# Recurrence weights split and rows squared during attention's first part, with five orders of loads, matmuls and tests changed

## The chip, the cores and the metric

The kernel runs on one core of a Trainium2 chip. The core has a matrix engine (TensorE, PE in the profile; PEld is its loading of weights), VectorE (DVE), ScalarE (ACT), GpSimd (POOL) and SyncE (SP), which here issues nearly all DMA transfers, from one queue in order. The metric is the device time of one execution in microseconds (us); lower is better.

## The reference

One decoder layer on 2048 tokens of 1024 features, in float32. The input is normalized and goes through one projection whose columns belong to three groups; their outputs are concatenated, projected, normalized and added to the input.

```python
hn = rms_norm(x, g_pre)
proj = hn @ w_in
rg_x, rg_g, da_q, da_k, da_v, da_g, xa_q, xa_g = jnp.split(proj, cuts, axis=-1)
xc = causal_depthwise_conv(rg_x, conv_w, conv_b)
y_rg = rg_lru(xc, w_rg_a, b_rg_a, w_rg_x, b_rg_x, lru_lambda) * jax.nn.silu(rg_g)
...
o = diff_attention(q, k, v, lam)
o = rms_norm(o, g_subln) * (1.0 - LAMBDA_INIT)
y_da = o.reshape(b_, s, DA_W) * jax.nn.silu(da_g)
oc = mem_cross_attention(xa_q.reshape(b_, s, XA_HEADS, XA_HEAD_DIM), km, vm)
y_xa = oc.reshape(b_, s, XA_W) * jax.nn.silu(xa_g)
y = jnp.concatenate([y_rg, y_da, y_xa], axis=-1) @ w_out
x = x + rms_norm(y, g_post)
```

`rg_lru` is a gated linear recurrence: two sigmoid gates from block-diagonal weights, then a scan along the tokens. `diff_attention` is causal, with 4 heads, two softmaxes per head of which one is subtracted with weight lambda. `mem_cross_attention` attends into 256 memory tokens.

## The kernel before

**Products in three parts.** A float32 operand is split into a high part in TensorE's rounded format and a low part, the rest. `split_weight` does this for weights: ScalarE copies the high part (L238), VectorE or GpSimd subtracts it (L239). `mm3` then runs three matmuls (high x high, low x high, high x low), each recorded by L198; transposes are L202.

**Projection.** The columns of `w_in` are grouped in 16 pairs of two 128-column blocks: eight of attention (qk, v, g), four of cross-attention (xa), four of the recurrence (rg). `project` runs twice: for chunks 0 and 1 of the 512-token chunks (the first half, pairs in their own order, so the rg pairs are pairs 12 to 15), then for chunks 2 and 3 (the second half, order `ORDER_B`, where rg pairs stand among the others). A pair is four blocks of 24 matmuls. In the first half each weight piece (four per pair) is loaded as `wraw`, split into `wp`, and stored to DRAM as `WD`; the second half loads `WD`. `w_conv` asks for pieces four or more ahead.

**Recurrence.** For each rg pair and chunk `ev_rg` evacuates the convolution's input (ScalarE, L592), convolves on VectorE (L597, L600), splits the result into `xchl` (VectorE L603, GpSimd L604), and makes the SiLU gate `rgg` (ScalarE, then VectorE L610). A little later `rg_gates` runs the gate matmuls `rgo`, their sigmoids on ScalarE, and the scan on VectorE (L637).

**Attention** is woven between the projection's matmuls by generators: `s_stream` makes scores and exponentials (`e`, in 12 buffers of the pool `pe`), weights and adds the two softmaxes (GpSimd L765, VectorE L766); `t_stream` transposes them (`pt`), splits them (ScalarE L806, VectorE L807) and multiplies by the values. `subln` normalizes each head with a matmul by ones. The order on PE is fixed by the program: a counter of recorded matmul time decides which generator goes next. The orders of the other engines and of the DMA queue come from a scheduler that follows dependences, buffers and priorities.

**Rows of x.** Chunk 0 is loaded and normalized first, and its transposes are woven with the first matmuls (`woven`). Rows of chunk 1 (`xrows`) and of the memory (`memx`) are loaded right behind it. Rows of chunks 2 and 3 are loaded at pair 13 (`next_x`), squared and summed on ScalarE (L283), and scaled on VectorE (L291).

**Output projection.** After the second half, `load_wout` splits the output weights in three groups (`woraw` to `wout` or `wo`); the token loop multiplies (`po`) in the order of groups 0, 2, 1.

Of the kernel before, what the change touches and what calls it, by code (L numbers as in the profile page):

```python
# [57 lines left out]
def hybrid_layer(  # L58
# [66 lines left out]
    ones_r = const.tile([128, 128], F32R, name="ones_r")  # L125
# [16 lines left out]
    def setup():  # L142
# [10 lines left out]
        nc.vector.tensor_scalar(ones_r, ident, 0.0, 1.0, op0=ALU.mult, op1=ALU.add)  # L153
# [164 lines left out]
    MEM0, WB0 = 8, 80  # L318
    wraw, wcv = {}, {}

    def w_load(*ids):
        for i in ids:
            if i < WB0:
                wraw[i] = praw.tile([128, 512], F32, tag="raw", name="wraw")
                nc.sync.dma_start(wraw[i], wsrc[i])

    def w_conv(*ids, eng=nc.gpsimd, pool=pw):
        for i in ids:
            if i < len(wsrc) and i not in wcv:
                w = wcv[i] = f4("wp", (128, 2, 2, 256), F32R, pool)  # L330
                if i >= WB0:

                    q = ORDER_B[(i - WB0) // 4]
# [5 lines left out]
                if not MEM0 <= i < MEM0 + 16:  # L339
                    q = i if i < MEM0 else i - 16  # L340
                    store(lambda w=w, q=q: nc.sync.dma_start(
                        WD[q // 4][q % 4], asf(w).rearrange("p a b c -> p (a b c)")), 4.0)
# [33 lines left out]
    for i in range(4):  # L376
        nc.sync.dma_start(xb[:, i].rearrange("p a b -> p (a b)"), x[CH + i * 128:CH + (i + 1) * 128, :])
    mrows = load_rows(mem, 2, "memx")
# [5 lines left out]
    def woven(c, rows):  # L384
# [6 lines left out]
        for kb in range(KB):  # L391
# [6 lines left out]
            if c == 0:  # L398
                if kb in (1, 2, 4, 6):
# [214 lines left out]
    def rg_gates(b, c, xc, xh, gs):  # L614
# [5 lines left out]
        ri = f4("ri", (128, 2, CH))  # L620
        for g in range(2):
            o = ps_s("rgo")
            mm3(o, state["rgh"][:, b, g, :], state["rgl"][:, b, g, :], xh[:, 0], xh[:, 1], True, True)
# [74 lines left out]
    def s_stream(jobs):  # L698

        q2s = {}  # L700

        def q2_load(i):
            if i < 2 * len(jobs) and i not in q2s:
                h, pr = jobs[i // 2]
                if has("qk", h, pr // 4):
                    q2s[i] = load_q2(h, 2 * pr + i % 2)
        due = now[0]
        for ij, (h, pr) in enumerate(jobs):
# [3 lines left out]
            while kready.get((h, pr // 4), 1e9) > now[0]:  # L712
# [119 lines left out]
    def subln(h, pr, A, B):  # L832
        c, j = divmod(pr, 2)
        s = ps_t("ss", (128, 256))
        mm(s, ones_r, B[:, 0, :], True, False)
        mm(s, ones_r, B[:, 1, :], False, True)
# [80 lines left out]
    xn = {}  # L917

    def next_x():
# [9 lines left out]
        for c in (2, 3):  # L929
            spawn(norm_steps(xn[c], SQ_GAP), 6.0 if c == 2 else 20.0)  # L930
# [8 lines left out]
    def start_b():  # L939
# [5 lines left out]
        (2, 0): start_attention,  # L945
        (13, 0): next_x,
# [12 lines left out]

    def load_wout(grp):  # L960
# [18 lines left out]
    project((2, 3), 80, ORDER_B, {(0, 0): start_b, (15, 2): last_pair})  # L979
# [118 lines left out]
```

## Time and profile before

| | |
|---|---|
| time, median of 3 runs (lowest to highest) | 1470.88 us (1470.23 to 1471.95) |
| the profiled execution's own time | 1467.53 us |
| its span, first to last instruction | 1465.7 us |
| TensorE matmuls busy | 1412.3 us, 96% |
| TensorE weight loads | 1199.2 us, 82% |
| VectorE, ScalarE, GpSimd busy | 61%, 53%, 33% |
| mean granted clock of TensorE | 0.994 |
| DMA | 234.37 MB, mean 160 GB/s |

Matmuls are pipelined and overlap the weight loads, so the two rows of TensorE don't add. A busy share is a mean over stages with different limits: what a stage is limited by is read from the waits in that stage. The granted clock is 1.00 at full speed (2.4 GHz) and 0.50 at the lower level (1.2 GHz).

### The profile page before, as it was taken

To read this page: it belongs to the slowest core of one execution; us is meant where nothing else is said; L and a number is where in the kernel's file an instruction comes from. 1 tells how busy PE (TensorE), PEld (TensorE's weight loads), DVE (VectorE), ACT (ScalarE), POOL (GpSimd) and SP (SyncE) were. 2 spreads that over 40 slices of the span, in tenths; PEclk is the share of its full clock that TensorE was granted. 3 is DMA by queue.
4 is the path that set the end of the run, shared out by engine and by line. 5 is a ranking of instruction groups with operands and counts; after the bars stand their busy time and mean duration, and the time that the engine had idled before them with its cause. 6 is when DMAs were issued, how large, how long until landed. Compare 5 with 4: busy or idle time off the path is not lost.

```text
span 1465.7 us, 21854 instructions
## 1 busy us (share of the span) xinstructions
PE 1412.3 (96%) x7568; PEld 1199.2 (82%) x7568; DVE 898.3 (61%) x1872; ACT 775.9 (53%) x1900; POOL 477.3 (33%) x568
## 2 busy tenths in 40 slices
PE   5999999999999899999999999999999999999997
PEld 3798889888887678888887898888877888888886
DVE  6531555676644876746547666757678777767222
ACT  6343544666547784745555545555566545554221
POOL 2031333344435632412213222212255333334221
PEclk9999999999999999999999999999999999999999
DMA  8689787745433348356324554232475334322231
GB/s 298 180 263 338 230 240 237 247 143 181 166 119 110 134 163 247 121 173 196 114 97 118 165 177 168 86 113 70 143 251 169 101 135 150 102 76 94 87 122 72
DMA packets 147870, 234.37 MB, mean 160 GB/s; under 512 B 12464, under 2 KB 82224, under 8 KB 147760
## 3 DMA queue, kind: packets, MB, share of 16 engines
q1 hardware_dynamic: 147616, 232.98, 48.8%
q8 instruction: 59, 0.97, 0.3%
q14 instruction: 51, 0.42, 0.1%
q10 hardware_dynamic: 144, 0.01, 0.0%
HBM read 142.76 MB, written 90.18 MB: 159 GB/s over the span
## 4 chain that ended last, share of the span: by engine, by line
PE 73%; DVE 9%; ACT 7%; DMA 4%; POOL 3%; issue 3%; SPq 1%; DVEq 0%; POOLq 0%; ACTq 0%
PE ip L198 36%; PE po L198 16%; PE s L198 7%; PE o L198 6%; PE pt L202 3%; PE xas L198 2%; DVE e L766 1%; DVE nm L740 1%; PE xao L198 1%; DMA q<-QD 1%; DVE xc L600 1%; PE rgo L198 1%; ACT e L742 1%; PE xat L202 1%; POOL e L765 1%
## 5 line engine op out<-in xcount | busy, mean ns | idle before, releaser
L198 PE MATMUL ip<-hnT,wp 128*128 128x512 f32 x2688 | 680.5, 397 | 6.9 <-DVE rgg L610 2.6
L198 PEld LDWEIGHTS ip<-hnT,wp 128*128 128x128 f32 x2688 | 496.0, 190 | 109.8 <-DVE hnT L307 4.5
L742 ACT ACTIVATE e<-s,nm 128x512 f32<-128x512 f32 (+3 forms) x320 | 200.1, 626 | 254.7 <-DVE nm L740 235.8
L740 DVE TENSOR_REDUCE nm<-s 128x1 f32<-128x512 f32 (+3 forms) x320 | 193.4, 605 | 37.4 <-PE s L198 33.1
L198 PE MATMUL po<-wout,yg 128*128 128x512 f32 x768 | 193.4, 393 | 5.0 <-POOL wout L239 2.4
L765 POOL TENSOR_SCALAR e<-e,f 128x512 f32<-128x512 f32 (+3 forms) x160 | 121.3, 773 | 235.5 <-DVE f L761 161.6
L198 PE MATMUL s<-kv,q 128*128 128x512 f32 (+3 forms) x640 | 182.9, 367 | 3.9 <-DMA q<-QD 2.4
L198 PEld LDWEIGHTS po<-wout,yg 128*128 128x128 f32 x768 | 141.1, 188 | 35.4 <-POOL wout L239 4.2
L766 DVE SCALAR_TENSOR_TENSOR e<-e,f 128x512 f32<-128x512 f32 (+3 forms) x160 | 138.0, 887 | 29.9 <-POOL e L765 29.7
L807 DVE TENSOR_TENSOR pthl<-pt,pthl 128x512 fp32r<-128x512 f32 (+1 forms) x144 | 94.5, 656 | 68.0 <-ACT pthl L806 67.5
L198 PE MATMUL o<-pthl,kv 128*128 128x256 f32 (+1 forms) x864 | 134.3, 290 | 1.0 <-DVE pthl L807 0.9
L198 PEld LDWEIGHTS s<-kv,q 128*128 128x128 f32 x640 | 114.5, 189 | 25.1 <-DMA q<-QD 3.0
L239 POOL TENSOR_TENSOR wp<-wraw,wp 128x512 fp32r<-128x512 f32 x67 | 91.1, 1368 | 127.1 <-ACT wp L238 110.8
L198 PEld LDWEIGHTS o<-pthl,kv 128*128 128x128 f32 x864 | 114.1, 189 | 4.5 <-DVE pthl L807 1.8
L806 ACT CAST pthl<-pt 128x512 fp32r<-128x512 f32 (+1 forms) x144 | 80.7, 561 | 55.2 <-PE pt L202 54.5
L239 POOL TENSOR_TENSOR yg<-yraw,yg 128x512 fp32r<-128x512 f32 x48 | 64.2, 1341 | 132.8 <-ACT yg L238 122.4
L198 PE MATMUL ip<-wp,hnT 128*128 128x256 f32 x768 | 99.7, 284 | 1.3 <-POOL wp L239 0.8
L198 PEld LDWEIGHTS ip<-wp,hnT 128*128 128x128 f32 x768 | 95.8, 191 | 3.0 <-POOL wp L239 1.0
L198 PE MATMUL po<-wo,yg 128*128 128x512 f32 x384 | 97.2, 392 | 0.0
L202 PE MATMUL pt<-ident,e 128*128 128x128 f32 x544 | 83.0, 272 | 3.3 <-DVE pthl L807 3.3
L198 PEld LDWEIGHTS po<-wo,yg 128*128 128x128 f32 x384 | 71.0, 188 | 14.3
L202 PEld LDWEIGHTS pt<-ident,e 128*128 128x128 f32 x544 | 66.9, 140 | 18.4 <-DVE pthl L807 3.8
(188 smaller groups left out, 1686.1 us busy)
## 6 DMA issues: line engine op xcount, KB each, us to landing
WD<-wp SPq DMA_DIRECT2D x64, 512.0 KB, 4.7
wp<-WD SPq DMA_DIRECT2D x64, 512.0 KB, 4.3
wraw<-in_w_in_dram SPq DMA_DIRECT2D x64, 256.0 KB, 3.4
q<-QD SPq DMA_DIRECT2D x128, 128.0 KB, 3.7
kv<-KD SPq DMA_DIRECT2D x24, 512.0 KB, 5.9
kv<-VD SPq DMA_DIRECT2D x24, 512.0 KB, 6.2
yraw<-YD SPq DMA_DIRECT2D x48, 256.0 KB, 2.7
QD<-qkhl SPq DMA_DIRECT2D x32, 256.0 KB, 3.5
```

What stands on the lines that cost most here:

```text
L198: nc.tensor.matmul(o, w, xx, start=start, stop=stop)
L202: nc.tensor.transpose(o, i, ident)
L239: eng.tensor_sub(lo, raw, asf(hi))
L600: nc.vector.scalar_tensor_tensor(xc[:, 0:CH], xr[:, k:k + CH], vec2[:, cw + k:cw + k + 1], xc[:, 0:CH], op0=ALU.mult, op1=ALU.add)
L740: nc.vector.tensor_reduce(out=nm[:, c, kc:kc + 1], in_=s[:, 0:w], op=ALU.max, axis=AX.X, negate=True)
L742: nc.scalar.activation(e[kc, c][:, 0:w], s[:, 0:w], AF.Exp, bias=nm[:, c, kc:kc + 1], accum_out=l[:, c, kc:kc + 1])
L765: nc.gpsimd.tensor_scalar(e2, e2, f[:, 1, kc:kc + 1], 1.0, op0=ALU.mult, op1=ALU.mult)
L766: nc.vector.scalar_tensor_tensor(e1, e1, f[:, 0, kc:kc + 1], e2, op0=ALU.mult, op1=ALU.add)
L806: nc.scalar.copy(hi[:, 0:n], t[:, 0:n])
L807: nc.vector.tensor_sub(lo[:, 0:n], t[:, 0:n], asf(hi[:, 0:n]))
```

## The change

1. **A new stage, `ahead`**, starts at pair 4 of the first half and takes three of the 12 `e` buffers until it ends. In each of 16 steps it loads one weight piece of the rg pairs and half a row block of chunks 2 and 3, splits the piece (ScalarE and GpSimd), stores both parts to `WD`, and squares and sums the row half on ScalarE. The rg pairs of the first half then load their pieces from `WD`. In `next_x` the rows of chunks 2 and 3, loaded again, are only scaled (`scale_rows`).
2. **The ones** of `subln` become one column, read 128 times.
3. **The start:** rows of chunk 1 are loaded during the fourth step of the first woven block, those of the memory behind that block.
4. **The gates' matmuls:** both gates' products with the high part run first, then both with the low part.
5. **Scores** of a job wait until 6.5 us of recorded time after its first query load.
6. **Output weights:** the four raw loads of group 2 are issued in the last quarter of the last pair, into free buffers.

```diff
-    ones_r = const.tile([128, 128], F32R, name="ones_r")
+    ones_r = const.tile([128, 1], F32R, name="ones_r")
...
-    MEM0, WB0 = 8, 80
+    MEM0, RG0, WB0 = 8, 64, 80
...
             if i < len(wsrc) and i not in wcv:
                 w = wcv[i] = f4("wp", (128, 2, 2, 256), F32R, pool)
-                if i >= WB0:
-
-                    q = ORDER_B[(i - WB0) // 4]
+                if i >= RG0:
+
+                    q = ORDER_B[(i - WB0) // 4] if i >= WB0 else (i - 16) // 4
                     nc.sync.dma_start(asf(w).rearrange("p a b c -> p (a b c)"), WD[q][i % 4])
                     continue
...
-    for i in range(4):
-        nc.sync.dma_start(xb[:, i].rearrange("p a b -> p (a b)"), x[CH + i * 128:CH + (i + 1) * 128, :])
-    mrows = load_rows(mem, 2, "memx")
+    mrows = []
...
             if c == 0:
+                if kb == 3:
+                    for i in range(4):
+                        t0 = CH + i * 128
+                        nc.sync.dma_start(xb[:, i].rearrange("p a b -> p (a b)"), x[t0:t0 + 128, :])
...
             w_conv(7, pool=p4)
+            mrows.extend(load_rows(mem, 2, "memx"))
...
+        os = [ps_s("rgo") for _ in range(2)]
         for g in range(2):
-            o = ps_s("rgo")
-            mm3(o, state["rgh"][:, b, g, :], state["rgl"][:, b, g, :], xh[:, 0], xh[:, 1], True, True)
+            mm(os[g], state["rgh"][:, b, g, :], xh[:, 0], True, False)
+            mm(os[g], state["rgl"][:, b, g, :], xh[:, 0], False, False)
+        for g in range(2):
+            o = os[g]
+            mm(o, state["rgh"][:, b, g, :], xh[:, 1], False, True)
...
                     q2s[i] = load_q2(h, 2 * pr + i % 2)
+                    landed[i] = now[0] + 6.5
...
-            while kready.get((h, pr // 4), 1e9) > now[0]:
+            while max(kready.get((h, pr // 4), 1e9), landed[2 * ij]) > now[0]:
...
-        mm(s, ones_r, B[:, 0, :], True, False)
-        mm(s, ones_r, B[:, 1, :], False, True)
+        ones = ones_r.to_broadcast([128, 128])
+        mm(s, ones, B[:, 0, :], True, False)
+        mm(s, ones, B[:, 1, :], False, True)
...
+    def ahead():
+
+
+        ssx = const.tile([128, 8, 2], F32, name="ssx")
+        while room["e"] < 3:
+            yield 0.4
+        room["e"] -= 3
+        for k in range(16):
+            raw = f2("wahead", (128, 512), F32R, pe)
+            nc.sync.dma_start(asf(raw), w_in[48 + k])
+            row = f2("xahead", (128, 512), pool=pe)
+            t0, j = 2 * CH + (k // 2) * 128, k % 2
+            nc.sync.dma_start(row, x[t0:t0 + 128, j * 512:j * 512 + 512])
+            yield 6.0
+            hi = f2("whi", (128, 512), F32R, pe)
+            nc.scalar.copy(hi, asf(raw))
+            nc.gpsimd.tensor_sub(raw, asf(raw), asf(hi))
+            yield 2.5
+            nc.scalar.activation(row, row, AF.Square, accum_out=ssx[:, k // 2, j:j + 1])
+            yield 1.0
+            for i, t in enumerate((hi, raw)):
+                nc.sync.dma_start(WD[12 + k // 4][k % 4][:, i * 512:i * 512 + 512], asf(t))
+            yield 3.5
+        room["e"] += 3
+        nc.gpsimd.tensor_add(rx, ssx[:, :, 0], ssx[:, :, 1])
+        rsqrt_mean(rx, rx, D)
+
+    def scale_rows(c):
+        for i, row in enumerate(xn[c]):
+            for p in row:
+                nc.vector.tensor_scalar_mul(p, p, rx[:, 4 * (c - 2) + i:4 * (c - 2) + i + 1])
+                yield SQ_GAP
...
-            spawn(norm_steps(xn[c], SQ_GAP), 6.0 if c == 2 else 20.0)
+            spawn(scale_rows(c), 6.0 if c == 2 else 20.0)
...
+        (4, 0): lambda: spawn(ahead()),
...
+    def last_raw():
+        for kb in range(4):
+            wo_load(2, kb)
+
+    project((2, 3), 80, ORDER_B, {(0, 0): start_b, (15, 2): last_pair, (15, 3): last_raw})
```

Three places show how the scheduler's lists move. The first is ScalarE in the rg pairs of the first half, about one chunk of one pair: `xr` is the convolution's input, `rgg` the SiLU gate, `rgo` and `ri` the two sigmoid gates, `junk` the squares, `wp` the weight splits. Before:

```order
L283 ACTIVATE junk,ss<-xrow 128x512 x2
L592 COPY xr<-ip 128x512
L238 CAST wp<-wraw 128x512
L283 ACTIVATE junk,ss<-xrow 128x512
L238 CAST wp<-wraw 128x512
L251 ACTIVATE rs<-rsv 128x4
L283 ACTIVATE junk,ss<-xrows 128x512
L252 ACTIVATE rs<-rs 128x4
L283 ACTIVATE junk,ss<-xrows 128x512
L260 ACTIVATE rgg<-ip 128x512
L283 ACTIVATE junk,ss<-xrows 128x512
L261 ACTIVATE rgg<-rgg 128x512
```

And in the changed kernel, from one pair's gates to the next:

```order
L637 ACTIVATE rga<-ri,nsp_249 128x512
L596 COPY xr<-ip 128x512
L638 ACTIVATE ri<-ri,nsp_250 128x512
L642 ACTIVATE ri<-ri,tinyb 128x512
L643 ACTIVATE ri<-ri 128x512
L260 ACTIVATE rgg<-ip 128x512
L261 ACTIVATE rgg<-rgg 128x512
L262 ACTIVATE rgg<-rgg 128x512
L260 ACTIVATE ri<-rgo,nbias 128x512 x2
L261 ACTIVATE ri<-ri 128x512 x2
L262 ACTIVATE ri<-ri 128x512 x2
```

The squares and the weight copies between the steps of the recurrence are gone; the gates' exponentials, logarithms and inverses follow each other in twos.

The second place is SP's DMA queue where attention begins, about 150 us into the span: `q` are query loads, `WD` weight stores, `GD` the store of an attention gate. Before:

```order
L341 DMA WD_180<-wp 128x1024
L325 DMA wraw<-in_w_in_dram 128x512
L692 DMA q_1711<-QD_98 128x2x128 x2
L341 DMA WD_181<-wp 128x1024
L325 DMA wraw<-in_w_in_dram 128x512
L506 DMA GD_151<-gs 128x512
L692 DMA q_1770<-QD_99 128x2x128 x2
```

And in the changed kernel:

```order
L328 DMA WD_180<-wp 128x1024
L325 DMA wraw<-in_w_in_dram 128x512
L939 DMA wahead<-in_w_in_dram 128x512
L942 DMA xahead<-in_x_dram 128x512
L328 DMA WD_181<-wp 128x1024
L700 DMA q_1721<-QD_98 128x2x128 x2
L510 DMA GD_151<-gs 128x512
L325 DMA wraw<-in_w_in_dram 128x512
L700 DMA q_1776<-QD_99 128x2x128 x2
```

The first two loads of the new stage and the second weight store now stand ahead of the first pair of query loads.

The third place is VectorE in the second half, about 766 to 777 us into the span: `xc` is the convolution, `e` the weighted sum of exponentials, `nm` the maxima of scores, `pthl` the split of transposed exponentials, `ri<-rga,carry,ri` the scan. Before:

```order
L766 SCALAR_TENSOR_TENSOR e<-e,f 128x512 x2
L740 TENSOR_REDUCE nm<-s 128x1
L766 SCALAR_TENSOR_TENSOR e<-e,f 128x512
L597 TENSOR_SCALAR xc<-xr,vec_243 128x512
L637 SCALAR_TENSOR_TENSOR ri<-rga,carry,ri 128x512
L740 TENSOR_REDUCE nm<-s 128x1
L600 SCALAR_TENSOR_TENSOR xc<-xr,vec_243,xc 128x512
L640 TENSOR_TENSOR ri<-ri,rgg 128x512
L600 SCALAR_TENSOR_TENSOR xc<-xr,vec_243,xc 128x512
L807 TENSOR_TENSOR pthl<-pt,pthl 128x512
```

And in the changed kernel:

```order
L601 TENSOR_SCALAR xc<-xr,vec_243 128x512
L775 SCALAR_TENSOR_TENSOR e<-e,f 128x512
L604 SCALAR_TENSOR_TENSOR xc<-xr,vec_243,xc 128x512
L749 TENSOR_REDUCE nm<-s 128x1
L604 SCALAR_TENSOR_TENSOR xc<-xr,vec_243,xc 128x512
L816 TENSOR_TENSOR pthl<-pt,pthl 128x512
L604 SCALAR_TENSOR_TENSOR xc<-xr,vec_243,xc 128x512
L749 TENSOR_REDUCE nm<-s 128x1
L607 CAST xchl<-xc 128x512
L775 SCALAR_TENSOR_TENSOR e<-e,f 128x512
L645 SCALAR_TENSOR_TENSOR ri<-rga,carry,ri 128x512
L816 TENSOR_TENSOR pthl<-pt,pthl 128x512
```

The convolution's first step moved ahead of a sum, and the scan moved from ahead of the first `pthl` to behind it.

## Rows read from the trace of the kernel before

**Rows 1.** Page, busy us (share of the span) and instructions of the engines

```profile
PE 1412.3 (96%) x7568; PEld 1199.2 (82%) x7568; DVE 898.3 (61%) x1872; ACT 775.9 (53%) x1900; POOL 477.3 (33%) x568
```

**Rows 2.** PE's waits by what ended them: us in total, times, longest

```profile
PE po L198 <- POOL wout L239: 2.4, 4, 0.7
PE po L198 <- ACT wout L238: 1.5, 1, 1.5
```

**Rows 3.** Timeline of PE: start, us, line, op, [idle before <-releaser]

```profile
480.67 0.73 PE L198 MATMUL rgo<-xchl,rgh 128*128 128x512 f32 x2 [1.40 <-POOL xchl L604]
487.45 8.45 PE L198 MATMUL ip<-hnT,wp 128*128 128x512 f32 x36 [1.25 <-DVE rgg L610]
511.16 0.73 PE L198 MATMUL rgo<-xchl,rgh 128*128 128x512 f32 x2 [1.16 <-POOL xchl L604]
```

**Rows 4.** Windows of 12 us: PE, PEld, DVE, ACT, POOL busy, clock, DMA, GB/s

```profile
478.00:490.00 12.00, 9.21 (x31) 6.49 (x30) 10.64 (x14) 11.44 (x26) 6.79 (x11) 0.86 0.55 188
773.00:785.00 12.00, 8.65 (x43) 6.91 (x42) 8.94 (x16) 8.22 (x19) 1.46 (x2) 0.86 0.39 122
```

**Rows 5.** Windows by stage, columns as in rows 4

```profile
150.00:455.00 305.00, 301.44 (x1665) 259.84 (x1665) 183.25 (x410) 170.75 (x431) 120.94 (x150) 1.00 0.60 193
455.00:515.00 60.00, 53.40 (x214) 41.30 (x213) 44.24 (x54) 45.39 (x100) 34.18 (x43) 0.95 0.37 126
515.00:1050.00 535.00, 527.34 (x2879) 450.65 (x2878) 349.40 (x690) 300.32 (x716) 139.16 (x185) 1.00 0.45 145
...
150.00:200.00 50.00, 50.00 (x241) 41.78 (x241) 28.51 (x63) 23.91 (x59) 17.39 (x20) 1.00 0.84 246
```

**Rows 6.** Groups by form, 455 to 515 us: xcount | busy us, mean ns

```profile
L600 DVE SCALAR_TENSOR_TENSOR xc<-xr,vec,xc 128x512 f32<-128x512 f32 x12 | 14.0, 1168 | 0.4
L239 POOL TENSOR_TENSOR wp<-wraw,wp 128x512 fp32r<-128x512 f32 x6 | 9.0, 1512 | 0.4 <-ACT wp L238 0.3
L283 ACT ACTIVATE junk<-xrow 128x512 f32<-128x512 f32 x8 | 5.0, 626 | 0.0
```

**Rows 7.** The same view, VectorE alone, 560 to 800 us

```profile
L600 DVE SCALAR_TENSOR_TENSOR xc<-xr,vec,xc 128x512 f32<-128x512 f32 x24 | 18.8, 784 | 0.4
```

**Rows 8.** Timeline of SP's queue and of PE, first query blocks

```profile
145.65 0.81 PE L198 MATMUL s<-kv,q 128*128 128x256 f32 x2 [2.38 <-DMA q<-QD]
...
152.42 0.94 SPq L692 DMA_DIRECT2D q<-QD  x2
...
160.48 0.62 PE L198 MATMUL s<-kv,q 128*128 128x512 f32 x2
```

**Rows 9.** Page, costliest groups: VectorE's weighted sum of exponentials

```profile
L766 DVE SCALAR_TENSOR_TENSOR e<-e,f 128x512 f32<-128x512 f32 (+3 forms) x160 | 138.0, 887 | 29.9 <-POOL e L765 29.7
```

**Rows 10.** Timeline of SP's queue and of ScalarE at the output projection

```profile
1083.92 10.68 SPq L969 DMA_DIRECT2D woraw<-in_w_out_dram  x5
...
1091.68 1.14 ACT L238 CAST wout<-woraw 128x512 fp32r<-128x512 f32 x2 [0.63 <-DMA woraw<-in_w_out_dram]
```

**Rows 11.** Timeline of GpSimd, VectorE and PE at 777 us

```profile
769.97 1.74 POOL L636 TENSOR_TENSOR ri<-ri 128x512 f32<-128x512 f32 x1
...
771.87 0.94 DVE L597 TENSOR_SCALAR xc<-xr,vec 128x512 f32<-128x512 f32 x1 [1.31 <-POOL xr L591]
776.43 0.68 DVE L807 TENSOR_TENSOR pthl<-pt,pthl 128x512 fp32r<-128x512 f32 x1
...
777.16 0.66 PE L202 MATMUL pt<-ident,e 128*128 128x128 f32 x4 [3.35 <-DVE pthl L807]
```

**Rows 12.** Timeline of VectorE and PE at the start

```profile
12.57 0.68 DVE L239 TENSOR_TENSOR wp<-wraw,wp 128x512 fp32r<-128x512 f32 x1
31.54 1.89 DVE L291 TENSOR_SCALAR memx<-memx,rs 128x512 f32<-128x512 f32 x2
...
34.15 1.19 PE L198 MATMUL ip<-hnT,wp 128*128 128x512 f32 x4 [1.38 <-DVE hnT L307]
```

**Rows 13.** Weight loads of the ones: duration ns min/median/max, first and last start

```profile
L198 PEld LDWEIGHTS ss<-sq,ones_r x64: 187/188/192, 172.1 to 1385.6; 128*128 128x128 f32 x64
```

More of the change, by code (lines that the diff above doesn't have):

```diff
@@ L152, in setup @@
         nc.vector.memset(tinyb, 1e-37)
-        nc.vector.tensor_scalar(ones_r, ident, 0.0, 1.0, op0=ALU.mult, op1=ALU.add)
+        nc.vector.tensor_scalar(ones_r, ident[:, 0:1], 0.0, 1.0, op0=ALU.mult, op1=ALU.add)
     def setup2():
@@ L322, in w_load, with w_store @@
         for i in ids:
-            if i < WB0:
+            if i < RG0:
                 wraw[i] = praw.tile([128, 512], F32, tag="raw", name="wraw")
                 nc.sync.dma_start(wraw[i], wsrc[i])
+    def w_store(w, q, delay):
+        store(lambda: nc.sync.dma_start(WD[q // 4][q % 4], asf(w).rearrange("p a b c -> p (a b c)")), delay)
     def w_conv(*ids, eng=nc.gpsimd, pool=pw):
@@ L339, in w_conv @@
                 if not MEM0 <= i < MEM0 + 16:
-                    q = i if i < MEM0 else i - 16
-                    store(lambda w=w, q=q: nc.sync.dma_start(
-                        WD[q // 4][q % 4], asf(w).rearrange("p a b c -> p (a b c)")), 4.0)
+                    w_store(w, i if i < MEM0 else i - 16, 4.0)
     def load_rows(src, n, name):
@@ L698, in s_stream @@
     def s_stream(jobs):
-        q2s = {}
+        q2s, landed = {}, {}
         def q2_load(i):
@@ L917, in hybrid_layer @@
     xn = {}
+    rx = const.tile([128, 8], F32, name="rx")
+    def ahead():
[27 more added lines that the diff above has]
+                yield SQ_GAP
     def next_x():
@@ L957, in y_granule, with wo_load @@
         return g
+    woraw = {}
+    def wo_load(grp, kb):
+        if (grp, kb) not in woraw:
+            raw = woraw[grp, kb] = f4("woraw", pool=pw if grp == 2 and kb == 3 else p4)
+            nc.sync.dma_start(raw, w_out[4 * grp + kb])
+        return woraw[grp, kb]
     def load_wout(grp):
@@ L967, in load_wout @@
         for kb in range(4):
-            raw = f4("woraw")
-            nc.sync.dma_start(raw, w_out[4 * grp + kb])
+            raw = wo_load(grp, kb)
             for j in range(2):
@@ L977, in last_pair @@
         load_wout(0)
-    project((2, 3), 80, ORDER_B, {(0, 0): start_b, (15, 2): last_pair})
+    def last_raw():
+        for kb in range(4):
+            wo_load(2, kb)
+    project((2, 3), 80, ORDER_B, {(0, 0): start_b, (15, 2): last_pair, (15, 3): last_raw})
     def y_ready(tt, grp):
```

## Prediction

> **What bounds the kernel now.** I read the busy times first: TensorE's matmuls stand at 1412.3 of 1465.7 us [rows 1], so some 53 us are idle. The change leaves the matmuls as they are, but for a few that change places, so it can only move waits. The table of PE's waits says which are large: 2.4 + 1.5 us, for instance, at the output projection's weights [rows 2]. The third reading was the timeline of PE through the last four pairs of the first half, the recurrence pairs: six waits of 0.5 to 1.4 us in 60 us, ended by VectorE or GpSimd, three of which stand in [rows 3]. There the clock matters too: around the waits at 480.67 and 777.16 a stretch of 12 us has a mean granted clock of 0.86 [rows 4], where the long stretches have 1.00 [rows 5]. At 0.86, 12 us hold 12 x 0.14 = 1.68 us less work, so such a wait costs itself plus 1.68.
>
> **Recurrence pairs: splits and squares taken out.** From 455 to 515 us PE is busy for 53.4 of 60 us, at a clock of 0.95 [rows 5]: 6.6 us of waits and 3.0 of clock, 9.6 in all. What is in the way: GpSimd's weight splits (1512 ns each) come ahead of the split of the convolved chunk, for which the gate matmuls wait; ScalarE squares rows of chunks 2 and 3 (16 x 0.62 us); and a VectorE convolution step takes 1168 ns [rows 6], against 784 ns in a stretch without weight splits [rows 7]. Sixteen splits and sixteen squares leave this part, as the first place of the order shows for ScalarE. The two gates' high halves also run first, so the low half is asked for two matmuls later. From 515 to 1050 us the same four pairs run for the second half, without splits, and PE loses 7.7 us in 535 [rows 5], 3.35 of it in one place (below). I leave 0.3 of the 9.6: **-9.3**, bounds -9.6 and -4 (more than half stays, as the sigmoids on ScalarE do).
>
> The Trainium skill ("SBUF — State Buffer", section "Who interferes with whom") says that a VectorE instruction with two SBUF inputs and a GpSimd instruction that reads SBUF shut each other out for a whole instruction. The 1168 against 784 ns agree with it.
>
> **The new stage in attention.** It runs from pair 4 to the end of pair 11, about 150 to 430 us: sixteen steps, each with two loads of 256 KB, a copy and a square on ScalarE (2 x 0.62 us), a subtraction on GpSimd (1.51 us) and two stores of 256 KB [rows 6]. ScalarE gets 20 us, where it is busy 171 of 305; GpSimd 24 us, with 121 of 305; the transfers 16 MB, or 55 GB/s beside 193, which brings a DMA share of 0.60 [rows 5] to 0.77. None is full. PE's order keeps its places but for some scores that run three matmuls later, so the three lent buffers of twelve do not hold the exponentials back. Queued behind the new transfers are the query loads: the second place of the order shows a pair of them behind two new loads and a store that stood behind them before. It was issued at 152.42, and its scores ran at 160.48 [rows 8]; 1 MB ahead of it takes 4 us at the 246 GB/s of that stretch [rows 5], so it still lands, with little left. The new test before a job's scores covers the job's first block alone; the wait of 2.38 us at 145.65 [rows 8] is a second block's, and stays. PE loses 305 - 301.4 = 3.6 us in this stage now [rows 5]. I price the new work at as much again, **+3.6**, with bounds 0 and +14.5: 24.2 us of subtractions that each stop VectorE whenever it has work, 183 of 305 us.
>
> By the skill's rule above the upper bound is smaller. In attention, of the work that reads two SBUF inputs, the weighted sum of exponentials is the largest (138 us of 1466 [rows 9]), and 24.2 x 138 / 1466 makes 2.3 us instead of 14.5.
>
> **Output projection.** PE waits 2.4 + 1.5 = 3.9 us for the second group's weights [rows 2]. Their raw loads stand among five issues that took 10.68 us from 1083.92 on, and ScalarE's first copy, at 1091.68, still waited for a transfer [rows 10]. The change issues these four loads in the last quarter of the last pair, ahead of key and value loads. The copies can then start at about 1086, and four subtractions of 1.5 us are through by 1092, when PE gets there: **-3.4**, bounds 0 and -3.9.
>
> **At 777 us** PE waited 3.35 us for a transposed block's subtraction on VectorE. VectorE had waited for GpSimd's copy of the halo until 771.87, behind a multiplication of 1.74 us on GpSimd, and came to the subtraction at 776.43 [rows 11]. The third place of the order shows the halo's consumer earlier, between two sums of exponentials, and the scan behind the subtraction. By the same rows the convolution starts near 770, and five or six VectorE steps of 0.6 to 0.9 us put the subtraction at 773.5 to 774: 0.5 us of wait stays, and no slow clock. 3.35 + 1.68 - 0.5 = **-4.5**, bounds +1 (the order is a scheduler's, not the chip's) and -5.0.
>
> **Start.** The rows of chunk 1 and of the memory are loaded later. The scaling of memory rows, 1.89 us on VectorE ahead of a block for which PE waits 1.38 [rows 12], moves behind it. But a weight split of 0.68 us [rows 12] now stands ahead of the fourth row's scaling, for which the first matmuls wait. Most of the one against half of the other: -1.4 + 0.3 = **-1.1**, bounds -1.4 and +0.7.
>
> **At nothing** stand the ones read as one repeated column (64 weight loads of 188 ns [rows 13], under matmuls; no row shows a repeated read, and twice the time would be 12 us of loads, with most still covered) and the recurrence weights' way back from DRAM, since they are asked for four pieces ahead, as those of the second half are, and PE has no wait for them there. VectorE's and ScalarE's lists also change in a few other places of the second half; I add **+1.4**, one wait like that at 480.67.
>
> Sum: -9.3 + 3.6 - 3.4 - 4.5 - 1.1 + 1.4 = -13.3. The profiled execution took 1467.5, so 1454.2; the median of the three runs, 1470.9, is 3.3 above it, hence **1457.5 us**, 0.9% less.
>
> **Rivals.**
> (1) The forecast, chance 0.62: 1457.5; its own range is 1450 (the gains at their bounds and half of the new losses) to 1463.
> (2) Only the recurrence pairs and the start gain, 0.18: one scheduler orders VectorE for all of the second half, and what 777 us and the projection give is lost beside them. -9.3 - 1.1 + 3.6 + 1.4 = -5.4: 1465.5. For it: both gains rest on an order alone. Against it: each has one late event in the rows that the new order takes away.
> (3) The work is only moved, 0.13: the subtractions stop VectorE for their full length in attention, +14.5 in place of +3.6. That leaves -2.4, 1468.5, which can't be told from no change. For it: 1168 against 784 ns. Against it: attention's first half already holds weight splits, and PE loses 3.6 us in it.
> (4) Slower, 0.07: the new transfers sit ahead of query loads in an in-order queue, and scores wait as they do at 145.65, 2.38 + 1.68 = 4.06 us each time. The gains sum to 18.3, less the 1.4; from the fifth such wait on (20.3) the kernel is slower by more than 2.9, and six make +7.5, 1478.4. For it: a DMA share of 0.84 from 150 to 200 us [rows 5]. Against it: later blocks are longer, and their loads are issued earlier.
>
> **Chances.** 0.2% (2.9 us) is about what a measurement of this kernel can tell from no change. Faster are (1) and (2), 0.80; the same (3), 0.13; slower (4), 0.07. The range 1449 to 1468 holds (1), (2) and the near half of (3).
>
> **What would show it.** Right: between 440 and 520 us no gate matmul that waits over 0.5 us, and a clock of 1.00; no wait over 1 us at the second group's weights; none of 3 us near 770; the first block's wait of 1.38 gone. Wrong: scores that wait for query loads between 150 and 430, a sum of exponentials well above its mean of 887 ns [rows 9] there, or new waits at transposed blocks in the second half.

## The result and the profile after

The changed kernel takes 1478.90 us (median of 5 runs, 1476.14 to 1481.34), the kernel before 1470.88 us beside it: ratio 1.0054, 95% interval 1.0032 to 1.0076, so 0.5% slower. The forecast was 1457.5, with a range of 1449 to 1468 and 0.07 for slower. The profiled execution has a span of 1478.6 us. The page's busy times of the engines are nearly those of [rows 1]:

```profile
PE 1418.8 (96%) x7568; PEld 1205.9 (82%) x7568; DVE 890.7 (60%) x1872; ACT 774.7 (52%) x1898; POOL 470.0 (32%) x562
```

TensorE's timeline in the same execution, its waits at the places that matter (start, us, line, operation, [idle before and what ended it]):

```profile
147.07 0.91 PE L198 MATMUL s<-kv,q 128*128 128x256 f32 x2 [2.79 <-DMA q<-QD]
...
227.26 0.58 PE L198 MATMUL ss<-sq,ones_r 128*128 128x256 f32 x1 [4.99 <-ACT sq L835]
270.91 2.93 PE L198 MATMUL ip<-hnT,wp 128*128 128x512 f32 x6 [3.88 <-DVE gs L509]
325.14 0.39 PE L198 MATMUL xas<-kmh,xaq 128*128 128x256 f32 x1 [1.47 <-ACT xaq L531]
```

And windows (PE, PEld, DVE, ACT, POOL busy, granted clock, DMA share, GB/s), which answer to [rows 4] and [rows 5]:

```profile
150.00:455.00 305.00, 286.15 (x1548) 242.75 (x1547) 183.66 (x411) 168.68 (x450) 123.02 (x155) 0.97 0.70 232
...
450.00:500.00 50.00, 50.00 (x229) 41.50 (x228) 25.20 (x39) 29.10 (x54) 17.21 (x23) 1.00 0.29 93
500.00:550.00 50.00, 50.00 (x237) 41.41 (x235) 31.01 (x40) 35.23 (x60) 18.27 (x24) 1.00 0.30 101
...
1050.00:1100.00 50.00, 50.00 (x277) 42.61 (x276) 38.37 (x79) 27.75 (x71) 20.67 (x25) 1.00 0.70 225
...
788.00:800.00 12.00, 9.85 (x49) 8.06 (x48) 12.00 (x15) 6.50 (x15) 5.02 (x5) 0.86 0.38 129
220.00:232.00 12.00, 6.79 (x38) 6.20 (x37) 5.95 (x16) 3.78 (x11) 3.90 (x6) 0.72 0.82 264
266.00:278.00 12.00, 8.12 (x32) 6.74 (x32) 5.01 (x15) 7.51 (x20) 2.71 (x4) 0.72 0.88 304
```

The gate pairs are repaired: PE is busy for all 100 us from 450 to 550, at a clock of 1.00. The output projection waits for nothing from 1050 to 1100. The loss is in attention: from 150 to 455 PE is busy for 286.15 us, where [rows 5] have 301.44, and two waits, of 4.99 and 3.88 us, stand where the kernel before has none. Around each the mean clock of 12 us is 0.72.

To compare kernels I cut each span at three places that all traces have: the first scores that wait for queries (145.65 before), the first cross-attention scores that wait (308.02), and the first wait at the transposes of chunk 3's rows (539.32). All figures are of one profiled execution each. Kernels that are alike in a stretch show how far one execution can be trusted: the first stretch differs by up to 7 us among the kernels below with the same start, the second by 1.3 us among the six without the new stage, and the last by 3.0 us between two kernels with the same lists (`xfer_only` and `xfer_small`).

| kernel | to 1st scores | attention to xa | xa and rg pairs | to the end | ratio to before |
|---|---|---|---|---|---|
| before | 145.7 | 162.4 | 231.3 | 926.4 | 1 |
| changed | 147.1 | 178.1 | 230.9 | 922.6 | 1.0054 |

So the second stretch loses 15.7 us: 8.9 of the two waits, and most of the rest by the clock (0.93 from 200 to 250 and again from 250 to 300, 3.5 us each). The third should have gained by the gate pairs, and gains 0.4. The fourth gains 3.8. What is lost ahead of the gate pairs are waits of cross-attention: PE is busy for 140.4 of the 150 us from 300 to 450 (146.9 before), and three of its waits there are:

```profile
385.67 0.50 PE L198 MATMUL xao<-xapt,vmh 128*128 128x512 f32 x1 [1.28 <-DVE xapt L569]
413.28 0.39 PE L198 MATMUL xas<-kmh,xaq 128*128 128x256 f32 x1 [1.40 <-ACT xaq L531]
431.63 0.50 PE L198 MATMUL xao<-xapt,vmh 128*128 128x512 f32 x1 [1.45 <-DVE xapt L569]
```

**How the first wait comes about.** The matmul at 227.26 sums the squares of an attention output `oa`. PE's last matmul of that output, ScalarE's timeline of the changed kernel, then GpSimd's, then ScalarE's of the kernel before, at the same output:

```profile
214.41 0.81 PE L198 MATMUL o<-pthl,kv 128*128 128x256 f32 x6
```

```profile
222.45 0.69 ACT L751 ACTIVATE e<-s,nm 128x512 f32<-128x512 f32 x1 [0.61 <-DVE nm L749]
...
223.13 0.19 ACT L765 ACTIVATE f<-f 128x4 f32<-128x4 f32 x1
223.22 0.36 ACT L832 COPY oa<-o 128x256 f32<-128x256 f32 x1
226.80 0.41 ACT L835 CAST sq<-oa 128x256 fp32r<-128x256 f32 x1 [3.22 <-POOL oa L833]
```

```profile
224.40 1.36 POOL L774 TENSOR_SCALAR e<-e,f 128x512 f32<-128x512 f32 x2 [4.28 <-DVE f L770]
225.72 1.04 POOL L833 TENSOR_TENSOR oa<-oa 128x256 f32<-128x256 f32 x1
```

```profile
213.28 0.19 ACT L742 ACTIVATION_READ_ACCUMULATOR e<-s,nm 128x1 f32 x1
213.37 0.36 ACT L823 COPY oa<-o 128x256 f32<-128x256 f32 x1
214.45 0.41 ACT L826 CAST sq<-oa 128x256 fp32r<-128x256 f32 x1 [0.72 <-POOL oa L824]
```

The copy runs 10 us later, 8 us after its input was complete (215.2), and waits for nothing when its turn comes: it stands later in ScalarE's list. Behind it, GpSimd's square has two scalings of exponentials ahead of it. The lists, which the scheduler fixes when the program is built, show it. ScalarE's before:

```
L742 ACTIVATE e,l<-s,nm 128x512
L823 COPY oa<-o 128x256
L826 CAST sq<-oa 128x256
L742 ACTIVATE e,l<-s,nm 128x512
L495 CAST vhl<-ip 128x256 x2
L742 ACTIVATE e,l<-s,nm 128x512
```

and after:

```
L751 ACTIVATE e,l<-s,nm 128x512
L499 CAST vhl<-ip 128x256 x2
L751 ACTIVATE e,l<-s,nm 128x512
L765 ACTIVATE f<-f 128x4
L832 COPY oa<-o 128x256
L835 CAST sq<-oa 128x256
```

This copy, of the third attention output, stands behind 22 exponentials before the change, and behind 24 after it. That number is given for the experiments below as the copy's place. (The second output's copy moved too, from 12 to 14, and PE doesn't wait for it.)

**The second wait** has a list behind it as well. The matmul at 270.91 needs an output buffer that VectorE frees when it makes an attention gate `gs`, for which ScalarE takes three steps (in the changed kernel L260, L261, L262). ScalarE's rows of one gate, after and before:

```profile
266.14 0.59 ACT L815 CAST pthl<-pt 128x512 fp32r<-128x512 f32 x1 [1.33 <-PE pt L202]
266.62 0.60 ACT L260 ACTIVATE gs<-ip 128x512 f32<-128x512 f32 x1
...
268.47 0.65 ACT L261 ACTIVATE gs<-gs 128x512 f32<-128x512 f32 x1
...
269.47 0.66 ACT L262 ACTIVATE gs<-gs 128x512 f32<-128x512 f32 x1
```

```profile
253.50 0.59 ACT L260 ACTIVATE gs<-ip 128x512 f32<-128x512 f32 x1
254.13 0.63 ACT L261 ACTIVATE gs<-gs 128x512 f32<-128x512 f32 x1
...
255.33 0.62 ACT L262 ACTIVATE gs<-gs 128x512 f32<-128x512 f32 x1
255.85 0.57 ACT L806 CAST pthl<-pt 128x512 fp32r<-128x512 f32 x1
```

Before, the gate stands ahead of the copy of transposed exponentials (`pthl`), with one exponential between its steps; after, it stands behind that copy, and more steps stand between its own. Which move of the lists came first, this doesn't tell.

### The profile page after: what moved, and what is told of

It is laid out like the page before. It is cut to its first block, busy times and chain, and to the rows that moved or that the text cites. A ratio compares the mean times of both kernels' runs of the same rounds, so it can differ in the third digit from the quotient of the medians.

```text
span 1478.6 us, 21945 instructions
## 1 busy us (share of the span) xinstructions
PE 1418.8 (96%) x7568; PEld 1205.9 (82%) x7568; DVE 890.7 (60%) x1872; ACT 774.7 (52%) x1898; POOL 470.0 (32%) x562
## 4 chain that ended last, share of the span: by engine, by line
PE 71%; DVE 8%; issue 6%; DMA 5%; ACT 5%; POOL 4%; SPq 1%; DVEq 0%; POOLq 0%; ACTq 0%
PE ip L198 35%; PE po L198 15%; PE s L198 7%; PE o L198 5%; PE pt L202 3%; DVE nm L749 1%; POOL wp L239 1%; PE rgo L198 1%; PE xao L198 1%; PE xas L198 1%; DMA q<-QD 1%; POOL e L774 1%; ACT e L751 1%; DVE e L775 1%; PE xat L202 1%
## 5 line engine op out<-in xcount | busy, mean ns | idle before, releaser
L239 POOL TENSOR_TENSOR wp<-wraw,wp 128x512 fp32r<-128x512 f32 x51 | 67.4, 1330 | 124.0 <-ACT wp L238 115.6
L198 PEld LDWEIGHTS ip<-wp,hnT 128*128 128x128 f32 x768 | 98.8, 196 | 4.6 <-ACT wp L238 2.3
L198 PEld LDWEIGHTS po<-wo,yg 128*128 128x128 f32 x384 | 71.6, 189 | 14.5
```

Source lines behind the costliest of these rows:

```text
L198: nc.tensor.matmul(o, w, xx, start=start, stop=stop)
L239: eng.tensor_sub(lo, raw, asf(hi))
```

## The experiments

Theory A: the new stage's transfers cost the time, either by their bytes on the chip (A1) or because they made the scheduler write other lists (A2). Theory B: its operations on ScalarE and GpSimd do. Rival C: the other five edits do. Every ratio is against the kernel before on the same chip. The diffs show the lines that matter; `...` stands for what is left out.

**Which part costs.** `no_ahead` undoes the stage, `only_ahead` has the stage and the one-column ones alone, and two kernels keep half of the stage each.

```diff
# no_ahead (only_ahead: the diff of the change without its other parts)
-    MEM0, RG0, WB0 = 8, 64, 80
+    MEM0, RG0, WB0 = 8, 80, 80
...
-        (4, 0): lambda: spawn(ahead()),
...
-            spawn(scale_rows(c), 6.0 if c == 2 else 20.0)
+            spawn(norm_steps(xn[c], SQ_GAP), 6.0 if c == 2 else 20.0)
# xfer_only, in ahead(); the rows' scale is set to 1
-            nc.scalar.copy(hi, asf(raw))
-            nc.gpsimd.tensor_sub(raw, asf(raw), asf(hi))
...
-            nc.scalar.activation(row, row, AF.Square, accum_out=ssx[:, k // 2, j:j + 1])
...
-            for i, t in enumerate((hi, raw)):
+            for i, t in enumerate((raw, raw)):
# arith_only, in ahead(); the operations read ident, repeated; the rg pairs load other pairs' pieces
-            nc.sync.dma_start(asf(raw), w_in[48 + k])
...
-            nc.sync.dma_start(row, x[t0:t0 + 128, j * 512:j * 512 + 512])
...
-                nc.sync.dma_start(WD[12 + k // 4][k % 4][:, i * 512:i * 512 + 512], asf(t))
```

`no_ahead`: 

> The changed kernel without its new stage: weights split and rows squared where they were before, the other five edits kept. The gate pairs' 9 to 10 us of loss come back between 450 and 550 us. Theory (the new stage is what costs): the wait of 4.99 us at the sums of squares and that of 3.88 us at the ip block (227 and 271 us in the changed kernel) are gone, and the time is 1465 to 1470 us. Rival (the other edits cost, the start's loads first of all): 1474 us or more, with those waits still there.

`only_ahead`: 

> The kernel before with the new stage and the one-column ones alone. Theory (the new stage costs some 20 us in its own stretch and gives 10 back at the gate pairs): 1478 to 1484 us. Rival (the other edits cost, the stage costs nearly nothing): 1458 to 1464 us.

`xfer_only`: 

> The changed kernel with the new stage's loads and stores alone: no copy, no subtraction, no square (the weights' parts and the rows' scale are then not the reference's). Theory A (the transfers, in one queue in order, hold up stores and loads that others wait for): 1474 to 1479 us, and the wait of some 5 us at the sums of squares near 227 us stays. Theory B (the operations stand ahead of urgent ones on ScalarE and GpSimd): 1456 to 1464 us.

`arith_only`: 

> The changed kernel with the new stage's copies, subtractions and squares alone, read from a constant, with the same buffers, and no load or store in the stage (the recurrence pairs then load other pairs' weights, as many bytes). Theory A (transfers): 1456 to 1464 us. Theory B (operations): 1474 to 1479 us, and the waits near 227 and 271 us stay.

| kernel | to 1st scores | attention to xa | xa and rg pairs | to the end | ratio (interval) | copy's place |
|---|---|---|---|---|---|---|
| no_ahead | 146.5 | 162.0 | 237.9 | 923.2 | 0.9997 (0.9981 to 1.0013) | 22 |
| only_ahead | 149.5 | 177.8 | 227.1 | 926.9 | 1.0057 (1.0036 to 1.0078) | 24 |
| xfer_only | 148.3 | 174.0 | 224.2 | 923.3 | 0.9979 (0.9962 to 0.9997) | 24 |
| arith_only | 148.0 | 164.1 | 231.0 | 922.7 | 0.9937 (0.9916 to 0.9958) | 22 |

The second stretch is a matter of the transfers: with them alone it is 174.0 long, with the operations alone 164.1 (162.4 before). TensorE's timeline with the transfers alone has the same two waits, to within 0.06 us, though nothing is split or squared:

```profile
225.34 0.58 PE L198 MATMUL ss<-sq,ones_r 128*128 128x256 f32 x1 [4.93 <-ACT sq L835]
268.61 2.93 PE L198 MATMUL ip<-hnT,wp 128*128 128x512 f32 x6 [3.88 <-DVE gs L509]
```

Theory B is wrong for these waits. But with the operations the third stretch is some 7 us longer (231.0 against 224.2), by waits at cross-attention scores and small ones; the gates' order and the test have a part in that, as later runs show. Neither half makes the kernel slower by itself; with both, the two losses stand against one gain at the gate pairs. The times of the halves, 1469.69 and 1464.81 us, fell between the ranges of the two theories, so the waits decide here and not the times. Rival C is wrong for the two waits too: without the stage both are gone. But `no_ahead` is slower than I expected under any theory but C, and the reason is in its third stretch, 6.6 us longer than before. Its windows and its longest wait there:

```profile
450.00:500.00 50.00, 41.14 (x175) 32.06 (x173) 29.66 (x36) 39.61 (x89) 27.91 (x34) 1.00 0.37 121
500.00:550.00 50.00, 46.00 (x212) 36.70 (x213) 37.81 (x49) 35.48 (x62) 20.77 (x27) 0.97 0.38 121
```

```profile
490.28 8.49 PE L198 MATMUL ip<-hnT,wp 128*128 128x512 f32 x36 [3.29 <-DVE rgg L614]
```

**Bytes or lists.** `xfer_small` separates A1 from A2: its transfers are cut after all lists are fixed, so that lists and waits are those of `xfer_only`, item by item. `grown` does the reverse: all of the change's work and bytes, in lists written for short transfers. `old_start` and `no_ahead_old_gates` test the start and the gates.

```diff
# xfer_small, once the scheduler is done (WD pieces of the rg pairs read from other pairs)
+    def _cut(p):
+        (s, n), rest = p.ap[0], p.ap[1:]
+        return _copy.replace(p, ap=[[s, n], [1, 32]], bass_ap=None)
...
+            _copy.replace(i, ins=[_cut(i.ins[0])], outs=[_cut(i.outs[0])])
# grown, in ahead() (likewise the other transfers); once the scheduler is done, [1, 32] becomes [1, 512]
-            nc.sync.dma_start(asf(raw), w_in[48 + k])
+            nc.sync.dma_start(asf(raw)[:, 0:32], w_in[48 + k][:, 0:32])
# old_start (likewise the rows of chunk 1)
-            mrows.extend(load_rows(mem, 2, "memx"))
...
-    mrows = []
+    mrows = load_rows(mem, 2, "memx")
# no_ahead_old_gates, against no_ahead, in rg_gates
         for g in range(2):
-            mm(os[g], state["rgh"][:, b, g, :], xh[:, 0], True, False)
-            mm(os[g], state["rgl"][:, b, g, :], xh[:, 0], False, False)
-        for g in range(2):
-            mm(o, state["rgh"][:, b, g, :], xh[:, 1], False, True)
+            mm3(o, state["rgh"][:, b, g, :], state["rgl"][:, b, g, :], xh[:, 0], xh[:, 1], True, True)
```

`xfer_small`: 

> The kernel with the new stage's transfers alone, whose 64 transfers are cut to a sixteenth of their bytes after the scheduler has set all lists, so that every engine's list and every wait is that of the kernel with the whole transfers (the recurrence pairs load other pairs' weights; the stage's result is not the reference's). Theory A1 (the transfers' bytes hold up others on the chip): the waits of 4.93 us at the sums of squares (225 us) and of 3.88 us at the ip block (269 us) are gone, and the time is 6 to 10 us below that of the whole transfers, 1460 to 1464 us. Theory A2 (the transfers made the scheduler write other lists, in which ScalarE copies the attention output behind two more exponentials): both waits stay within 0.5 us of their length, and the time is 1467 to 1471 us.

`grown`: 

> The changed kernel with all of its work and bytes, but the scheduler sees the new stage's transfers at a sixteenth of their bytes and writes its lists for that; the transfers get their full length afterwards. The third copy of an attention output then stands behind 23 exponentials (22 before the change, 24 after). Theory A1 (bytes on the chip): no faster than the changed kernel, 1477 to 1481 us. Theory A2 (lists): the wait of 4.99 us at 227 us is shorter by 2 us or more, 1468 to 1475 us.

`old_start`: 

> The changed kernel with the loads of chunk 1 and of the memory where they were before. If the start's gain of 2 us reaches the end: 2 us slower than the changed kernel, about 1481 us. If it is lost where the weights arrive near 103 and 147 us: within 1.5 us of it, with the first matmuls of pair 2 at the same time, 103 to 104 us, with a shorter wait.

`no_ahead_old_gates`: 

> The changed kernel without its new stage and with the gates' matmuls in their old order; start, scores' test, output weights and one-column ones are kept. If the new order of the gates costs where the splits still stand (PE was busy 87 of 100 us from 450 to 550 without the new stage, 92 before): 92 of 100 again and 1467 to 1470 us. If not: 1472 to 1474 us as without the new stage alone.

| kernel | to 1st scores | attention to xa | xa and rg pairs | to the end | ratio (interval) | copy's place |
|---|---|---|---|---|---|---|
| xfer_small | 149.3 | 174.5 | 224.1 | 920.3 | 0.9964 (0.9949 to 0.9980) | 24 |
| grown | 145.2 | 166.1 | 232.2 | 923.8 | 1.0003 (0.9987 to 1.0019) | 23 |
| old_start | 152.4 | 177.8 | 232.0 | 921.9 | 1.0062 (1.0039 to 1.0085) | 24 |
| no_ahead_old_gates | 148.4 | 161.8 | 235.3 | 924.2 | 0.9963 (0.9948 to 0.9978) | 22 |

TensorE's timeline of `xfer_small`, and its window around the first wait:

```profile
226.33 0.52 PE L198 MATMUL ss<-sq,ones_r 128*128 128x256 f32 x1 [4.91 <-ACT sq L835]
270.95 2.93 PE L198 MATMUL ip<-hnT,wp 128*128 128x512 f32 x6 [3.87 <-DVE gs L509]
```

```profile
220.00:232.00 12.00, 6.80 (x36) 6.31 (x36) 5.94 (x16) 2.91 (x9) 3.77 (x5) 0.77 0.53 165
```

With a sixteenth of the bytes, and a DMA share of 0.53 in that window in place of 0.71 in `xfer_only`, the waits are 4.91 and 3.87 us. It is the lists: A2 holds, and A1 is wrong for these waits; the time, 1468.56 us, is that of A2 as well. `grown` agrees: the same work and bytes in other lists are 0.5% faster than the changed kernel, and neither wait is there (others, up to 1.84 us, are). The start is worth nothing that can be told: 1.0062 against 1.0054. Where the splits still stand, the gates' new order costs 0.34%, and those two intervals don't meet. Which rows carry it I can't say: the third stretch is 2.6 us longer, but a wait of 2.86 us at the line of the 3.29 us stays in the old order too.

**What in the lists, and the repair.** An attention output's copy needs a buffer from a pool that it shares with, among others, the loads of its gate (`gt`) and of queries, and the gate's load asks first. On the lists alone, without a run, one buffer less or a higher priority for the copy left its place at 24; taking the gate's load out of the pool made it 23, both loads 22. I read this as the scheduler handing out a pool's buffers in turn, with a load that in its reckoning waits for the queue holding up the copy behind it; the lists show the effect, not the reckoning. The next kernels have it on the chip.

```diff
# own_pool
-    p2 = ctx.enter_context(tc.tile_pool(name="p2", bufs=9))
+    p2 = ctx.enter_context(tc.tile_pool(name="p2", bufs=6))
+    pq = ctx.enter_context(tc.tile_pool(name="pq", bufs=3))
...
-        t = f2("q2", (128, 2, 2, 128), F32R)
+        t = f2("q2", (128, 2, 2, 128), F32R, pq)
...
-            gt = f2("gt", (128, 256))
+            gt = f2("gt", (128, 256), pool=pq)
...
# _old_gates: as above; _no_test, in s_stream:
-            while max(kready.get((h, pr // 4), 1e9), landed[2 * ij]) > now[0]:
+            while kready.get((h, pr // 4), 1e9) > now[0]:
# wo_start: no_ahead with old gates and no test; own_pool_before: the pools alone;
# own_pool_no_stage, own_pool_old_start: own_pool_old_gates_no_test without the stage, or with the old start
```

`own_pool`: 

> The changed kernel with three of the nine small buffers set apart for the loads of queries and gates, so that the buffer of an attention output is no longer handed out behind a gate load that waits for the queue; the third output's copy then stands behind 22 exponentials, as before the change. Theory A2 (lists, through the order in which this pool hands out buffers): the wait of 4.99 us at 227 us is gone or under 1 us, and the time is 1468 to 1474 us. Rival A3 (the place of that copy is one symptom of many; the lists differ in other places as much): other waits of the same sum stand between 147 and 310 us, and the time is 1477 us or more.

`own_pool_old_gates`: 

> The same with the gates' matmuls in their old order. Without the new stage the old order was 5 us faster. If it is the splits beside it that make the new order dear, it costs nothing here, where they are gone: within 1.5 us of the own-pool kernel. If the new order is dear by itself: 4 to 6 us faster than that.

`own_pool_old_gates_no_test`: 

> The same again, and without the test of recorded time before a job's scores, so that PE's order is that of before. The kernel before with the new stage alone lost 5 us less between the first cross-attention scores and chunk 3's transposes than the changed kernel with the old start. If the test is why: 4 to 6 us faster than the kernel with the test. If it is the gates: no faster than that (within 1.5 us).

`wo_start`: 

> The kernel before with the start's loads, the early output weights and the one-column ones alone; PE's order is that of before. By the stretches measured so far: the output projection's waits of 3.9 us gone (-3.4), the start's 2 us lost at 103 and 147 us: 1467 to 1470 us. If the test of recorded time is what gained in the kernel without stage and new gates (1467.6): 1471 us or more.

`own_pool_before`: 

> The kernel before with only the buffers of query and gate loads set apart. If the separate buffers repair what the new stage's transfers did to the lists: no change, 1470 to 1474 us, since the copies of attention outputs already stand early in the lists of before. If separate buffers are a gain by themselves: 1462 to 1466 us.

`own_pool_no_stage`: 

> The fastest kernel so far (1460 us: new stage, separate buffers, start's loads, early output weights, old gates, no test) without the new stage. If the stage is worth what its stretches say once the lists are repaired (7 to 9 us back at the gate pairs, less 2 to 4 us in attention): 1465 to 1468 us. If the stage is worth nothing: 1459 to 1462 us.

`own_pool_old_start`: 

> The fastest kernel so far with the start's loads as before. If the start's 2 us are lost again where the first weights arrive: within 1.5 us of 1460 us. If they reach the end: 1462 us or more.

| kernel | to 1st scores | attention to xa | xa and rg pairs | to the end | ratio (interval) | median us |
|---|---|---|---|---|---|---|
| own_pool | 148.7 | 164.5 | 231.3 | 923.3 | 0.9955 (0.9941 to 0.9969) | 1464.81 |
| own_pool_old_gates | 147.0 | 164.7 | 228.5 | 922.6 | 0.9940 (0.9917 to 0.9963) | 1461.66 |
| own_pool_old_gates_no_test | 145.1 | 163.6 | 225.2 | 922.4 | 0.9928 (0.9901 to 0.9954) | 1460.04 |
| wo_start | 145.8 | 162.5 | 231.5 | 923.4 | 0.9968 (0.9951 to 0.9985) | 1466.42 |
| own_pool_before | 150.4 | 162.9 | 234.1 | 927.0 | 1.0002 (0.9985 to 1.0020) | 1472.81 |
| own_pool_no_stage | 148.4 | 161.6 | 234.3 | 923.7 | 0.9979 (0.9964 to 0.9993) | 1469.45 |
| own_pool_old_start | 147.6 | 164.7 | 226.9 | 921.6 | 0.9937 (0.9914 to 0.9960) | 1463.68 |

The copy of `own_pool` on ScalarE's timeline, and its windows:

```profile
216.08 0.37 ACT L833 COPY oa<-o 128x256 f32<-128x256 f32 x1
```

```profile
200.00:250.00 50.00, 49.61 (x351) 46.18 (x349) 30.24 (x71) 26.80 (x72) 23.33 (x23) 1.00 0.92 300
250.00:300.00 50.00, 47.96 (x247) 40.44 (x248) 32.06 (x72) 33.30 (x88) 20.63 (x26) 1.00 0.90 313
```

Three buffers set apart make the changed kernel 1% faster (1.0054 to 0.9955). Both waits are gone and the clock is 1.00, though the DMA share is now 0.92 and 0.90, higher than in the changed kernel (0.78 and 0.88). By themselves the pools give nothing (1.0002). So they repair what the stage did to the lists. Against the same kernel without the stage (0.9979 to 0.9928) the stage is worth 0.5%, 7.5 us, and the two intervals don't meet. That comparison flatters the stage: where the splits still stand among the gate pairs, the separate pools cost 2.8 us in the third stretch, in both pairs of kernels that show it (231.3 to 234.1, and 231.5 to 234.3). A wait of 3.39 us at a gate pair is new in both kernels with the pools and without the stage; in `own_pool_no_stage`:

```profile
507.62 10.04 PE L199 MATMUL ip<-hnT,wp 128*128 128x512 f32 x36 [3.39 <-DVE rgg L615]
```

Against `wo_start`, which has the shared pool (0.9968), stage and pools together are worth 0.4%, and there the intervals just meet (0.9951 to 0.9985, 0.9901 to 0.9954).

`own_pool` and `wo_start` were faster than I expected, by 3.2 and 0.6 us, and `own_pool_no_stage` was 1.5 us slower. `own_pool_old_gates` fell between its two expectations, 3.2 us below `own_pool`; without the test it is 1.6 us less again. `own_pool_old_start` fell in the range of a start that reaches the end, but beside another run of the kernel before. By the ratios the old gates and the missing test are 0.15% and 0.12% faster, which the intervals don't tell from nothing; nor is the start (0.9937 against 0.9928). `own_pool_old_gates_no_test` is the fastest kernel here, 0.7% below the kernel before and 1.2% below the changed one.

## Why the prediction was wrong

**The step that failed** is the price of the new stage, +3.6 with an upper bound of 14.5. It cost 15.7 us in the second stretch (15.4 in `only_ahead`), and the runs put that down to the lists that its transfers brought. A second step failed beside it: the gates' new order stood among the gains and the test had no price, and together they cost some 6 us in the third stretch (below). Of the 26.2 us between the summed terms (-13.3) and the two profiled spans (+12.9), the second stretch holds 12.1 and the third 8.9. I reckoned with what the stage occupies: busy time on ScalarE and GpSimd, bytes, and places on PE and in the queue. "PE's order keeps its places" was right for the stage, and of no help: ScalarE's and GpSimd's lists, which the order of instructions shows as plainly, I read for the gate pairs and not for attention. There the copy of an attention output stands two exponentials later. The bound was one of contention, and no bound on what another list can do.

**Recurrence pairs, -9.3.** Right at the gate pairs: PE has no wait and a full clock from 450 to 550. With the lists repaired the third stretch is 9.1 us shorter with the stage than without it (225.2 and 234.3); 2.8 of these are the pools' own cost without the stage, and against `wo_start` (231.5) it is 6.3. In the changed kernel 7 of them are lost again ahead of the gate pairs, and in `arith_only` too. That loss isn't the operations' busy time either: the fastest kernel has the same operations and 225.2 us. What differs is the gates' order and the test, and the lists with them. With separate pools the stretch is 231.3 us with both, 228.5 with the old gates and 225.2 without the test too (one execution each; two kernels that differ in the start alone are 1.7 apart there). The loss doesn't need the stage either: without it the stretch is 237.9 us with both (`no_ahead`) and 231.5 with neither (`wo_start`). With the transfers alone, without the stage's splits and squares, it isn't there (224.2). So the gates' order and the test cost some 6 us beside that work, wherever it stands; by which list, the runs don't tell.

**The stage itself, +3.6.** With the lists repaired the second stretch is 163.6 us, against 161.6 without the stage: +2.0. So the term's size holds for what the work occupies. That rival (3), subtractions that stop VectorE for their full length, is wrong is shown by `arith_only`: 164.1, +1.7 against before. VectorE's rows from 150 to 440 us, first the changed kernel, then the kernel before:

```profile
L775 DVE SCALAR_TENSOR_TENSOR e<-e,f 128x512 f32<-128x512 f32 (+3 forms) x35 | 32.9, 963 | 15.2 <-POOL e L774 15.2
```

```profile
L766 DVE SCALAR_TENSOR_TENSOR e<-e,f 128x512 f32<-128x512 f32 (+3 forms) x35 | 29.9, 877 | 10.4 <-POOL e L765 10.4
```

The sums of exponentials grow by 3.0 us in all. It is the operations: with the transfers alone a sum takes 880 ns, with the operations alone 999, in the fastest kernel 1019 (5.0 us in all). The estimate of 2.3 us that I had worked out by a rule of the Trainium skill ("SBUF — State Buffer", section "Who interferes with whom") is of that size, and somewhat low.

**Rival (4)** ended at 1478.4, and the time is 1478.9, but its mechanism didn't happen: the only wait for queries is the old one, now 2.79 us, and no wait of 4 us was added there. The agreement is luck.

**Output projection, -3.4.** Right: no wait from 1050 to 1100. The last stretch is 923.4 us with the early loads (`wo_start`) and 926.4 and 926.9 in the kernel before and `only_ahead`, without them. A little later a transposed block waits longer than before, 1.9 us in every kernel with the early loads and 0.7 to 0.8 in those without:

```profile
1121.49 0.74 PE L198 MATMUL o<-pthl,kv 128*128 128x256 f32 x4 [1.89 <-DVE pthl L816]
```

**At 777 us, -4.5.** Too large. The wait, at 793.55 now, is 2.15 us and the clock of its window still 0.86; 1.2 us are won. With the old gates it stays (3.35 us in `wo_start`, and in `no_ahead_old_gates` with the test), and so the gates' order has shortened it. The same order brings a wait of its own, of 1.85 to 2.13 us in all kernels that have it and of nothing in those with the old gates:

```profile
685.33 0.89 PE L198 MATMUL s<-kv,q 128*128 128x512 f32 x2 [1.87 <-ACT e L751]
...
793.55 0.66 PE L202 MATMUL pt<-ident,e 128*128 128x128 f32 x4 [2.15 <-DVE pthl L816]
```

That is of the size of the +1.4 for other orders in the second half. The last stretch as a whole gained 3.8, where these three terms add to -6.5.

**Start, -1.1.** Open. The first matmuls of pair 2 start 2 us earlier (98.61, 100.68 before), but most of it is lost at their next weights, for which PE waits 2.10 us (0.50 before):

```profile
103.03 0.50 PE L198 MATMUL ip<-wp,hnT 128*128 128x256 f32 x2 [2.10 <-ACT wp L238]
```

The first scores, which wait for a transfer, come at 145.1 to 149.3 us with the new start and at 145.7 to 152.4 with the old one, and no pair of ratios tells them apart. The wait that was priced at +0.3 did come: 1.24 us at 15.93, in every kernel with the new start.

**At nothing.** Right for the ones (64 loads with a median of 188 ns, as in [rows 13]) and for the recurrence weights' way back, where PE has no wait. One slip in the sums: (1)'s range began at 1450, but from the median its terms give 1453.5 (1470.9 - 19.9 + 2.5).

## What to carry to other kernels

In a kernel whose lists a scheduler writes, the price of new work is not only what it occupies: compare the list of every engine over the whole stretch in which the work runs, and look for the urgent short step (a copy that frees or feeds TensorE) that now stands behind others. A wait that keeps its length when the suspected bytes or operations are taken out, with the lists held, is the list's. Where loads that may wait share a pool of buffers with the results of urgent steps, try to set some buffers apart: here that undid the loss. In lists that were good it gave nothing, and cost 2.8 us at the gate pairs.

## What the runs showed that I had not expected

The chip took 16 MB of new transfers nearly for free: cut to a sixteenth, the same lists are 0.15% faster (0.9979 to 0.9964, within their intervals), and in `own_pool` and the fastest kernel PE is busy for 49.6 and 49.9 of the 50 us from 200 to 250, at a DMA share of 0.92. The clock made the waits dear: 8.9 us of waits in attention brought about 7 us of slow clock with them, more than the 1.68 for each wait that I had read from [rows 4].
